# A two-group SSD encoder layer on one core: order of the early loads, 14 more raw tiles in h's own space, ada visits of four

## Chip, cores, metric

The kernel runs on one core of one Trainium2 chip. The metric is device time in microseconds, the median of the timed runs: 3281.73 us for the kernel before (three runs, 3269.22 to 3285.26). All arithmetic is float32; the large matmuls split each operand into a float32r part and a rest and run three products.

## What is computed

One adaLN-modulated mixer layer for 256 prompt rows and 32 sample rows (288 rows, N), D = 4096. Cut to what matters:

```python
mod = silu(c) @ w_ada + b_ada                    # w_ada 4096 x 12288
shift, scale, gate = split(mod, 3)
h = layer_norm(x) * (1 + scale) + shift
proj = h @ w_in                                  # w_in 4096 x 18528
u_pool, g_pool, z, xbc, dt_raw = split(proj)
pool_out = pool_mixer(u_pool) * silu(g_pool)
xs, B, C = split(silu(causal_conv(xbc)))
y = ssd_scan(xs, softplus(dt_raw + dt_bias), A, B, C) + d_skip * xs
ssd_out = grouped_rms_norm(y * silu(z)) * ssd_norm_w
o = concat(pool_out, ssd_out) @ w_out            # w_out 8192 x 4096
x_new = layer_norm(alpha * x + gate * o) * ln_g + ln_b
```

Outputs are x_new for both row groups and the new states of pool, convolution and SSD.

## The kernel before

Everything is transposed: features lie on partitions, the 288 rows are the moving columns. A weight tile of 128 x 128 is stationary, h (or the mixed activations) moves. `hH` and `hL` [128, 32, 288] hold the float32r part and the rest of h, k-tile by k-tile.

Weights come in steps of 512 KB (128 x 1024 floats) into raw tiles, from a first-in-first-out list `rawfree`: four of `rawS` for the whole kernel and five of `rawA` for the first phase. `loads()` hands a free raw tile to the next step in the list and issues its load on SyncE's queue (SP); where the tile's last reader has not finished yet, SP waits there, in order. A w step is converted by ScalarE (`hi`, three buffers), then VectorE computes the rest (`lo`, two buffers) and gives the raw tile back; PE then runs, for each of four blocks of 128 columns and each k-tile, three matmuls hi x hH, hi x hL, lo x hH. An ada step is used raw: c is the stationary operand, w_ada moves.

In the first phase (phase A) h doesn't exist as a whole. It is made in ten slabs of k-tiles, `SLABS = [2]*4 + [4]*6`. Slab s needs its columns of shift and scale, 16 ada steps for a slab of two and 32 for a slab of four (L416 loads them), then `h_slab` (L576): x rows again from memory (L580, L574), normalised by VectorE, transposed by PE, modulated into `ht`, split into `hH` and `hL`. With them the slab's part of 13 blocks of w_in (set A, 49 column tiles) is accumulated into 49 slots of `arena`. Lines 683 to 697 interleave the ada steps of the slabs to come with the w steps: FIRST steps ahead, due LEAD = 4 w steps before a slab begins, in visits of VISIT = 4 ada steps, or of two while the first two slabs run. Before a slab's first w step the program waits in its building (`flush`) for `h_done`. After phase A the full h is there, and the rest of w_in, the pool and SSD work and w_out follow.

The order of instructions on every engine is the order in which the program is built. `run()` (L319) walks the steps; a planner (`tick`) advances background generators between steps, and inside a generator `yield n` means: not before n ticks. For the step at t, conversions are emitted for w steps up to t + 5 + VISIT (L328). `finish` (in `ada_steps`) takes the ada accumulator out by ScalarE (`ev`), sums it by PE (`pR`) and adds b_ada on VectorE (`mod`). At the start twelve loads of x feed 24 `bn_stats`; `x_done` (L561) runs `ln_stats` and `params`, which transposes the parameters that ScalarE's queue loaded ahead of everything else.

Nearly all instructions are issued through one helper and carry the line L101 in the trace; they are told apart by their tiles.

Of the kernel before, what the change touches and what calls it, by code (L numbers as in the profile page):

```python
# [9 lines left out]
F32 = mybir.dt.float32  # L10
# [145 lines left out]
def trunk(ctx, tc, A):  # L156
# [10 lines left out]

    hH = cp.tile([P, KT, N], F32R, name="hH")
    hL = cp.tile([P, KT, N], F32R, name="hL")
    arena = cp.tile([P, NSLOT, N], F32, name="arena")  # L170
# [19 lines left out]
    def pbank(tag):  # L190
        return ps.tile([P, 512], F32, tag=tag, name=tag)
# [37 lines left out]
    def bg(g):  # L229
        pending.append(Gen(g))  # L230
# [71 lines left out]

    rawA_ids = set()

    def raw_free(st):
        if st.rawid in rawA_ids and state.get("noA"):
            return
        rawfree.append((st.rawid, st.raw))
# [3 lines left out]
    def loads():  # L312
        while state["load"] < len(steps) and rawfree:
            st = steps[state["load"]]
            st.rawid, st.raw = rawfree.popleft()
            st.custom(st.raw)
            state["load"] += 1

    def run():  # L319
        for t, st in enumerate(steps):  # L320
            if st.pre:
                st.pre()
            if st.kind != "a" or not steady[0]:
                tick()
            loads()
            ahead = 0
            i = t
            while i < min(state["load"], t + 5 + VISIT) and ahead < HB:  # L328
                if steps[i].kind == "w":
                    if steps[i].hi is None:  # L330
                        split_hi(steps[i])
                    if steps[i].lo is None and ahead < LB:
                        split_lo(steps[i])
                    ahead += 1
                i += 1
            loads()
            T.t = max(T.t, 1.46 * t)
            st.pe(st)
            if st.kind != "w":
                raw_free(st)  # L340
            if st.after:
                st.after()
# [28 lines left out]
    def hmv(kt):  # L371
        return hH[:, kt % KT, :], hL[:, kt % KT, :]

# [91 lines left out]
    def ini(rows, n):  # L465
        inis.append(Slot(free.popleft()))
        return inis[-1].ap[0:rows, 0:n]
# [3 lines left out]
    S.dma_start(c2[32:64, :], A["c_sample"].rearrange("o (k c) -> (o k) c", c=P))  # L471
    p4 = ini(P, P)
    S.dma_start(p4[0:48, :], A["ssd_norm_w"].rearrange("o (k c) -> (o k) c", c=P))
    S.dma_start(p4[48:64, :], A["pool_scale"].rearrange("o (k c) -> (o k) c", c=P))
    S.dma_start(p4[64:96, :], A["ln_g"].rearrange("o (k c) -> (o k) c", c=P))
    S.dma_start(p4[96:128, :], A["ln_b"].rearrange("o (k c) -> (o k) c", c=P))
    ba = ini(96, P)
    S.dma_start(ba, A["b_ada"].rearrange("o (k c) -> (o k) c", c=P))
    cw = ini(P, 2 * P).rearrange("p (a c) -> p a c", a=2)
    S.dma_start(cw, A["conv_w"].rearrange("o r (t c) -> (o r t) c", c=P).rearrange("(a p) c -> p a c", p=P))  # L480
    cb = ini(64, P)
    S.dma_start(cb, A["conv_b"].rearrange("o (t c) -> (o t) c", c=P))
    sv = ini(96, 2 * P).rearrange("p (a c) -> p a c", a=2)
    S.dma_start(sv, A["state_conv"].rearrange("o b r (t c) -> (o b r t) c", c=P).rearrange("(a p) c -> p a c", p=96))
    sp = ini(120, 2 * P).rearrange("p (a c) -> p a c", a=2)
    S.dma_start(sp, A["state_pool"].rearrange("o b r (t c) -> (o b r t) c", c=P).rearrange("(a p) c -> p a c", p=120))
    S.dma_start(sc96[:, 0:1], A["dt_bias"].rearrange("o h -> h o"))
    S.dma_start(sc96[:, 1:2], A["a_log"].rearrange("o h -> h o"))
    S.dma_start(sc96[:, 2:3], A["d_skip"].rearrange("o h -> h o"))

    pt = pbank("pT")
# [3 lines left out]
    V.scalar_tensor_tensor(th, th, 1.0, pt[:, 0:64], ALU.add, ALU.mult)  # L495
    V.tensor_scalar(cT.rearrange("p k s -> p s k"), th.rearrange("p (s k) -> p s k", s=2), 0.5, None, ALU.mult)
    def params():
        pt = pbank("pR")
        T.transpose(pt[:, 0:P], p4, ident)
        T.transpose(pt[:, P:P + 96], ba, ident[0:96, 0:96])  # L500
        V.tensor_copy(prm, pt[:, 0:P])
        V.tensor_copy(badaT, pt[:, P:P + 96])
        V.tensor_scalar(prm[:, 48:64], prm[:, 48:64], 0.5, None, ALU.mult)
        pt = pbank("pY")
        T.transpose(pt[:, 0:128], cw[:, 0, :], ident)
        T.transpose(pt[:, 128:256], cw[:, 1, :], ident)
        T.transpose(pt[:, 256:320], cb, ident[0:64, 0:64])
        T.transpose(pt[:, 320:416], sv[:, 0, :], ident[0:96, 0:96])
        T.transpose(pt[:, 416:512], sv[:, 1, :], ident[0:96, 0:96])
        cvf = convT.rearrange("p r t -> p (r t)")  # L510
        V.tensor_scalar(cvf[:, 0:320], pt[:, 0:320], 0.5, None, ALU.mult)
        V.tensor_copy(cvf[:, 320:512], pt[:, 320:512])
        pt = pbank("pT")
        T.transpose(pt[:, 0:120], sp[:, 0, :], ident[0:120, 0:120])
        T.transpose(pt[:, 120:240], sp[:, 1, :], ident[0:120, 0:120])
        V.tensor_copy(spT.rearrange("p r t -> p (r t)"), pt[:, 0:240])
        for sl in inis:
            sl.rel()
# [24 lines left out]
    def ln_stats():  # L543
        tmp = pa.tile([P, 3, 4], F32, name="lnt")
        for i, (src, rows) in enumerate(xsrc):
            r = slice(0, rows)
            V.bn_aggr(stats[r, i, :], bst[r, i, :, :])
            v, q, y, w = (tmp[r, i, k:k + 1] for k in range(4))
            rs = stats[r, i, 1:2]
            V.tensor_scalar(v, rs, LN_EPS, None, ALU.add)  # L550
            S.activation(q, v, AF.Sqrt)
            V.reciprocal(y, q)
            V.tensor_tensor(w, y, y, ALU.mult)
            V.tensor_tensor(w, w, v, ALU.mult)
            V.tensor_scalar(w, w, -0.5, 1.5, ALU.mult, ALU.add)
            V.tensor_tensor(rs, y, w, ALU.mult)

        for r in (32, 64, 96):
            V.tensor_copy(stats[r:r + 32, 2, :], stats[0:32, 2, :])

    def x_done():  # L561
        ln_stats()
        params()

# [5 lines left out]

    def sample_rows(t, k0, nk):

        for q in range(nk):
            nc.sync.dma_start(t[NS * q:NS * q + NS, :], A["x_sample"][0][:, (k0 + q) * P:(k0 + q + 1) * P])  # L574

    def h_slab(k0, nk):  # L576
        xc = pa.tile([P, 2, 512], F32, tag="xc", bufs=1, name="xc")
        xq = pa.tile([P, P], F32, tag="xq", bufs=1, name="xq")
        for i, (src, rows) in enumerate(xsrc[0:2]):
            nc.sync.dma_start(xc[:, i, 0:nk * P], src[:, k0 * P:(k0 + nk) * P])  # L580
        sample_rows(xq, k0, nk)
        yield
        for i in range(2):
# [7 lines left out]
        for tg in ("pT", "pY"):  # L591
            yield from lock(tg)
        hq = pa.tile([P, P], F32, tag="hq", bufs=1, name="hq")
        for q in range(nk):
# [10 lines left out]
            V.tensor_scalar(ht[:, NP:N], hq[:, NS * q:NS * q + NS], mod[:, 32 + kt, 1:2], mod[:, kt, 1:2], ALU.mult, ALU.add)  # L605
            S.copy(hH[:, kt, :], ht)
            V.tensor_tensor(hL[:, kt, :], ht, hH[:, kt, :].bitcast(F32), ALU.subtract)
            if q % 2:
# [47 lines left out]
    for s, nk in enumerate(SLABS):  # L656
# [7 lines left out]

        def pre(k0=k0, nk=nk):
            bg(h_slab(k0, nk))
        SL[0].pre = pre
        astream += SL
        need.append((len(wstream), len(astream)))
# [12 lines left out]

    early = need[2][0]
    a = paced = need[0][1] + FIRST
    steps.extend(astream[:a])
    for i, w_ in enumerate(wstream):
        steps.append(w_)
        want, due = paced, a
        for w0, a1 in [x for x in need if x[0] > i][:2]:
            left = w0 - LEAD - i  # L690
            want = max(want, a1 if left <= 0 else paced + (a1 - paced) / (left + 1))
            due = max(due, a1 if left <= 0 else 0)
        paced = want
        visit = 2 if i < early else VISIT
        upto = max(due, a + int(paced - a) // visit * visit)
        steps.extend(astream[a:upto])
        a = upto
# [3 lines left out]
    def noA():  # L701
        state["noA"] = True
        keep = [r for r in rawfree if r[0] not in rawA_ids]
        rawfree.clear()
        rawfree.extend(keep)
    st = steps[steps.index(lastA[0]) - 10]
# [557 lines left out]
    def mix_split(kt):  # L1264
        sl = mload.pop(kt)
        q = kt % KT
        S.copy(hH[:, q, :], sl.ap)
        V.tensor_tensor(hL[:, q, :], sl.ap, hH[:, q, :].bitcast(F32), ALU.subtract)
        sl.rel()
# [302 lines left out]
```

## Time and profile before

| | us |
|---|---|
| median of three timed runs | 3281.73 |
| the profiled execution, its time | 3289.41 |
| the profiled execution, span from first to last instruction | 3287.6 |
| PE busy / VectorE / ScalarE / GpSimd | 3139.0 / 1910.2 / 1306.8 / 122.5 |
| mean granted TensorE clock | 0.989 |
| bytes moved | 718.29 MB, 218 GB/s in the mean |

All times in the trace count from the start of the span. PE is TensorE's matmul side, DVE VectorE, ACT ScalarE, POOL GpSimd, SP SyncE; a name with q is the engine's queue, where DMAs are issued. Busy times are spans of instructions; matmuls overlap in the engine, so a group's mean is longer than what one adds. In the chain of waits, x24 on a piece is the number of instructions in it.

### The profile page before, as it was taken

To read this page: it belongs to the slowest core of one execution; us is meant where nothing else is said; L and a number is where in the kernel's file an instruction comes from. 1 tells how busy PE (TensorE), PEld (TensorE's weight loads), DVE (VectorE), ACT (ScalarE), POOL (GpSimd) and SP (SyncE) were. 2 spreads that over 40 slices of the span, in tenths; PEclk is the share of its full clock that TensorE was granted. 3 is DMA by queue.
4 is the path that set the end of the run, shared out by engine and by line. 5 is a ranking of instruction groups with operands and counts; after the bars stand their busy time and mean duration, and the time that the engine had idled before them with its cause. 6 is when DMAs were issued, how large, how long until landed. Compare 5 with 4: busy or idle time off the path is not lost.

```text
span 3287.6 us, 59637 instructions
## 1 busy us (share of the span) xinstructions
PE 3139.0 (95%) x24003; PEld 2911.8 (89%) x24003; DVE 1910.2 (58%) x3335; ACT 1306.8 (40%) x1953; POOL 122.5 (4%) x232
## 2 busy tenths in 40 slices
PE   4988999999999999999999999999899999999998
PEld 1866888888999999999999999989799999999998
DVE  3555555555767746655667656566555533554764
ACT  1422222222434434444444544444444433533543
POOL 0000000000000000000000000000000000000000
PEclk9999999999999999999999999999999999999999
DMA  8878888888565666666666766666766666755554
GB/s 273 287 253 294 312 296 296 299 297 282 149 188 172 200 200 190 197 215 199 212 199 199 217 207 204 197 191 197 230 192 223 205 202 203 244 183 167 170 167 135
DMA packets 428883, 718.29 MB, mean 218 GB/s; under 512 B 34335, under 2 KB 135151, under 8 KB 428607
## 3 DMA queue, kind: packets, MB, share of 16 engines
q1 hardware_dynamic: 418432, 696.39, 66.3%
q0 software_dynamic: 8480, 17.38, 1.4%
q8 instruction: 188, 3.08, 0.4%
q10 hardware_dynamic: 1695, 0.72, 0.1%
q14 instruction: 88, 0.72, 0.1%
HBM read 693.21 MB, written 21.06 MB: 217 GB/s over the span
## 4 chain that ended last, share of the span: by engine, by line
PE 84%; DVE 6%; DMA 6%; ACT 2%; issue 2%; SPq 1%; ACTq 0%; POOL 0%; DVEq 0%; POOLq 0%
PE acc L101 75%; PE ada L101 4%; PE pT L101 3%; DVE lo L101 2%; DMA rawS<-w_in 2%; PE pY L101 2%; DMA rawA<-w_in 1%; DVE arena L101 1%; PE pR L101 1%; DVE cacc L101 1%; ACT hi L101 1%; DMA arena<-spill 1%; DVE ht L101 1%; ACT hH L101 1%; DMA xq<-x_sample 0%
## 5 line engine op out<-in xcount | busy, mean ns | idle before, releaser
L101 PE MATMUL acc<-hH,hi 128*128 128x288 f32 x6688 | 2006.2, 300 | 40.3 <-DVE arena L101 35.9
L101 PE MATMUL acc<-hH,lo 128*128 128x288 f32 x6688 | 1983.9, 297 | 32.3 <-DVE lo L101 31.7
L101 PE MATMUL acc<-hL,hi 128*128 128x288 f32 x6688 | 1981.7, 296 | 0.1
L101 PEld LDWEIGHTS acc<-hH,hi 128*128 128x128 f32 x6688 | 1265.8, 189 | 143.3 <-ACT hi L101 56.1
L101 DVE TENSOR_TENSOR lo<-rawS,hi 128x1024 fp32r<-128x1024 f32 x751 | 914.3, 1218 | 808.6 <-PE acc L101 476.1
L101 PEld LDWEIGHTS acc<-hH,lo 128*128 128x128 f32 x6688 | 1265.0, 189 | 39.6 <-DVE lo L101 38.4
L101 ACT CAST hi<-rawS 128x1024 fp32r<-128x1024 f32 x751 | 784.5, 1046 | 1291.5 <-PE acc L101 570.4
L101 PEld LDWEIGHTS acc<-hL,hi 128*128 128x128 f32 x6688 | 1266.3, 189 | 1.0 <-DVE hL L101 0.5
L101 DVE TENSOR_TENSOR arena<-acc,arena 128x288 f32<-128x288 f32 x441 | 190.4, 454 | 109.9 <-PE acc L101 109.3
L101 ACT CAST hi<-rawA 128x1024 fp32r<-128x1024 f32 (+2 forms) x99 | 99.9, 1011 | 263.1 <-DMA rawA<-w_in 162.0
L101 PE MATMUL ada<-rawS,cT 128*2 128x512 f32 (+1 forms) x1076 | 162.4, 563 | 27.2 <-ACT ev L101 15.9
L101 DVE TENSOR_TENSOR lo<-rawA,hi 128x1024 fp32r<-128x1024 f32 (+2 forms) x99 | 116.2, 1174 | 114.5 <-ACT hi L101 42.6
L101 PE MATMUL ada<-rawA,cT 128*2 128x512 f32 (+1 forms) x716 | 113.5, 539 | 8.1 <-DMA rawA<-w_ada 4.6
L101 ACT ACTIVATE m<-m 128x896 f32<-128x896 f32 x96 | 91.5, 953 | 56.4 <-DVE m L101 54.7
L101 DVE SCALAR_TENSOR_TENSOR cacc<-cbuf,convT,cacc 128x291 f32<-128x291 f32 x192 | 100.3, 522 | 6.8
L101 DVE TENSOR_TENSOR arena<-arena 128x288 f32<-128x288 f32 (+1 forms) x224 | 100.0, 454 | 5.6 <-ACT arena L101 0.7
L101 PEld LDWEIGHTS ada<-rawS,cT 128*2 128x2 f32 x1076 | 21.8, 83 | 63.9 <-issue 27.3
L101 ACT COPY arena<-acc 128x288 f32<-128x288 f32 x177 | 63.9, 403 | 32.7 <-PE acc L101 32.6
L101 ACT ACTIVATE arena<-arena 128x288 f32<-128x288 f32 (+1 forms) x89 | 38.8, 442 | 73.1 <-DVE arena L101 73.0
L101 PE MATMUL pT<-cst,arena 128*128 128x128 f32 (+5 forms) x237 | 46.0, 281 | 18.3 <-DMA arena<-ln_b 6.9
L101 DVE TENSOR_TENSOR hL<-arena,hH 128x288 fp32r<-128x288 f32 x64 | 26.9, 456 | 59.5 <-ACT hH L101 59.4
L101 PEld LDWEIGHTS ada<-rawA,cT 128*2 128x2 f32 x716 | 18.3, 84 | 45.5 <-issue 21.8
(198 smaller groups left out, 1459.1 us busy)
## 6 DMA issues: line engine op xcount, KB each, us to landing
rawS<-w_in SPq DMA_DIRECT2D x426, 512.0 KB, 4.5
rawS<-w_out SPq DMA_DIRECT2D x256, 512.0 KB, 3.7
rawS<-w_ada SPq DMA_DIRECT2D x241, 512.0 KB, 4.4
rawA<-w_ada SPq DMA_DIRECT2D x143, 512.0 KB, 5.5
rawA<-w_in SPq DMA_DIRECT2D x86, 512.0 KB, 6.1
rawS<-w_in SPq DMA_DIRECT2D x114, 256.0 KB, 3.7
m<-acd SPq DMA_DIRECT2D x48, 448.0 KB, 5.0
spill<-arena POOLq DMA_DIRECT2D x64, 144.0 KB, 4.2
```

Source lines behind the costliest of these rows:

```text
L101: return f(out, *a, **k)
```

## The change

Six things are changed.

1. hH and hL become eight tiles each, of four k-tiles. Until a group of k-tiles is made, its space serves as raw tiles: 14 more in `rawfree` (groups 1 to 7, two each). `retire` takes those of groups that the coming slab needs out of the list when the slab's first ada step comes up, and `h_slab` waits in building until they are out of use.
2. Parameters that only later work needs are loaded by GpSimd's queue in a background generator `params`, queued at the last ada step of slab 1, into four arena slots. At the start ScalarE issues only the constants and c; b_ada is loaded and transposed in `params_first`, after the statistics.
3. The x rows of each slab are loaded by GpSimd's queue and first touched six ticks later rather than one.
4. Before the first w step conversions are emitted only up to t + 3.
5. Visits of four ada steps in all slabs.
6. `ln_stats` computes the three row groups' factors at once.

```diff
-    hH = cp.tile([P, KT, N], F32R, name="hH")
-    hL = cp.tile([P, KT, N], F32R, name="hL")
+    early = {(nm, b): cp.tile([P, 4 * N], F32, tag="%s%d" % (nm, b), name="e%s" % nm)
+             for b in range(KT // 4) for nm in ("hH", "hL")}
+    made = {}
+    def hpart(nm, kt):
+        b = kt // 4
+        if (nm, b) not in made:
+            made[nm, b] = cp.tile([P, 4, N], F32R, tag="%s%d" % (nm, b), name=nm)
+        return made[nm, b][:, kt % 4, :]
...
     def raw_free(st):
-        if st.rawid in rawA_ids and state.get("noA"):
+        inuse.discard(st.rawid)
+        if st.rawid in retired:
             return
...
+    def retire(ids):
+        retired.update(ids)
+        keep = [r for r in rawfree if r[0] not in retired]
+        rawfree.clear()
+        rawfree.extend(keep)
...
-            while i < min(state["load"], t + 5 + VISIT) and ahead < HB:
+            while i < min(state["load"], t + (5 + VISIT if t >= state["first"] else 3)) and ahead < HB:
...
-    p4 = ini(P, P)
-    S.dma_start(p4[0:48, :], A["ssd_norm_w"].rearrange("o (k c) -> (o k) c", c=P))
...
-    S.dma_start(sc96[:, 2:3], A["d_skip"].rearrange("o h -> h o"))
...
+    def params_first():
+        ba = ini(96, P)
+        S.dma_start(ba, A["b_ada"].rearrange("o (k c) -> (o k) c", c=P))
+        pt = pbank("pR")
+        T.transpose(pt[:, P:P + 96], ba, ident[0:96, 0:96])
+        V.tensor_copy(badaT, pt[:, P:P + 96])
...
     def params():
+        pi = []
+        for _ in range(4):
+            sl = yield from galloc()
+            pi.append(sl)
...
+        G.dma_start(p4[0:48, :], A["ssd_norm_w"].rearrange("o (k c) -> (o k) c", c=P))
...
+        yield 8
+        yield from lock("pR")
         pt = pbank("pR")
         T.transpose(pt[:, 0:P], p4, ident)
...
     def x_done():
         ln_stats()
-        params()
+        params_first()
...
+    for b in range(1, 8):
+        for q, nm in enumerate(("hH", "hL")):
+            rawfree.append((200 + 2 * b + q, early[nm, b][:, 0:1024]))
...
-            nc.sync.dma_start(xc[:, i, 0:nk * P], src[:, k0 * P:(k0 + nk) * P])
-        sample_rows(xq, k0, nk)
-        yield
+            G.dma_start(xc[:, i, 0:nk * P], src[:, k0 * P:(k0 + nk) * P])
+        sample_rows(xq, k0, nk, G)
+        yield 6
...
+        while any(200 <= i < 200 + 2 * ((k0 + nk + 3) // 4) for i in inuse):
+            yield "w"
...
         def pre(k0=k0, nk=nk):
+            retire([i for b in range(8) if 4 * b < k0 + nk + 2 for i in (200 + 2 * b, 201 + 2 * b)])
             bg(h_slab(k0, nk))
         SL[0].pre = pre
+        if s == 1:
+            SL[-1].pre = lambda: bg(params())
...
-        visit = 2 if i < early else VISIT
-        upto = max(due, a + int(paced - a) // visit * visit)
+        upto = max(due, a + int(paced - a) // VISIT * VISIT)
```

## Rows read from the trace of the kernel before

**Rows 1.** The page, part 1: busy us (share of the span) x instructions of each engine.

```profile
PE 3139.0 (95%) x24003; PEld 2911.8 (89%) x24003; DVE 1910.2 (58%) x3335; ACT 1306.8 (40%) x1953; POOL 122.5 (4%) x232
```

**Rows 2.** Windows: busy us of PE, PEld, DVE, ACT, POOL; then clock, DMA share, GB/s.

```profile
72.00:312.00 240.00, 215.22 (x1692) 178.42 (x1692) 128.10 (x237) 74.15 (x120) 0.00 (x0) 0.94 0.84 278
...
411.00:511.00 100.00, 96.71 (x738) 82.64 (x737) 55.54 (x90) 28.59 (x32) 0.00 (x0) 1.00 0.87 300
...
1000.00:1500.00 500.00, 489.32 (x3728) 465.27 (x3728) 321.45 (x615) 223.65 (x368) 26.35 (x49) 0.99 0.64 197
```

**Rows 3.** Timeline to 72 us: start, us, engine, instruction [idle before <- releaser].

```profile
6.91 0.34 PE L101 MATMUL pT<-cst,arena 64*128 64x64 f32 x1 [6.91 <-DMA arena<-ln_b]
...
13.61 1.28 ACT L101 ACT_TABLE_LOAD   x1 [13.61 <-DMA arena<-state_pool]
...
15.53 4.84 DVE L101 BATCH_NORM_STATS2 bst<-rawS 128x6 f32<-128x512 f32 x8
...
25.92 1.03 PE L101 MATMUL ada<-rawS,cT 128*2 128x256 f32 x8 [9.82 <-DVE bst L101]
...
48.77 1.03 PE L101 MATMUL ada<-rawS,cT 128*2 128x256 f32 x8 [0.48 <-DMA rawS<-w_ada]
...
62.14 1.04 ACT L101 CAST hi<-rawA 128x1024 fp32r<-128x1024 f32 x1 [5.43 <-DMA rawA<-w_in]
...
63.09 0.37 ACT L101 COPY ev<-ada 128x256 f32<-128x256 f32 x1
...
71.98 0.40 PE L101 MATMUL acc<-hH,hi 128*128 128x288 f32 x1 [2.48 <-ACT hH L101]
```

**Rows 4.** Windows of five microseconds with the DMA engines full, columns as above.

```profile
45.00:50.00 5.00, 3.73 (x32) 0.32 (x24) 0.00 (x0) 0.00 (x0) 0.00 (x0) 1.00 1.09 362
...
365.00:370.00 5.00, 5.00 (x42) 4.83 (x44) 2.42 (x4) 2.10 (x2) 0.00 (x0) 1.00 1.05 401
```

**Rows 5.** Waits of SP's queue, 72 to 312 us: total us, times, longest.

```profile
SPq L392 <- DVE lo L101: 68.8, 21, 7.7
SPq L392 <- DVE arena L101: 29.9, 12, 4.2
```

**Rows 6.** The chain of waits in phase A: start, us, what.

```profile
82.86 0.97 PE ada L101 x16
83.83 6.54 PE acc L101 x48
...
177.96 6.33 DMA xc<-x_prompt
...
221.95 6.48 DMA rawA<-w_in
...
307.36 0.27 ACT hq L101
...
312.55 3.44 PE acc L101 x24
```

**Rows 7.** DMA issues: engine, count, KB each, median us to landing.

```profile
spill<-arena POOLq DMA_DIRECT2D x64, 144.0 KB, 4.2
...
arena<-conv_w ACTq DMA_DIRECT2D x1, 128.0 KB, 6.4
...
arena<-b_ada ACTq DMA_DIRECT2D x1, 48.0 KB, 3.8
```

**Rows 8.** Windows inside the stretch of 72 to 312 us.

```profile
165.00:190.00 25.00, 18.02 (x133) 16.83 (x133) 15.20 (x32) 5.33 (x8) 0.00 (x0) 0.92 0.67 214
...
215.00:235.00 20.00, 11.29 (x79) 8.19 (x79) 8.20 (x19) 5.33 (x8) 0.00 (x0) 0.88 0.87 298
```

**Rows 9.** Windows around the x rows' arrival, slabs of four: the first two and the last of five.

```profile
320.00:332.00 12.00, 8.85 (x61) 7.45 (x54) 6.03 (x10) 2.18 (x3) 0.00 (x0) 0.88 0.85 283
...
420.00:436.00 16.00, 14.46 (x108) 12.60 (x109) 10.02 (x19) 3.58 (x4) 0.00 (x0) 1.00 0.87 295
...
721.00:737.00 16.00, 13.02 (x97) 11.16 (x98) 9.38 (x16) 3.57 (x4) 0.00 (x0) 1.00 0.77 250
```

More of the change, by code (lines that the diff above doesn't have):

```diff
@@ L303, in trunk @@
     rawA_ids = set()
+    retired = set()
+    inuse = set()
     def raw_free(st):
-        if st.rawid in rawA_ids and state.get("noA"):
+        inuse.discard(st.rawid)
+        if st.rawid in retired:
             return
@@ L315, in loads @@
             st.rawid, st.raw = rawfree.popleft()
+            inuse.add(st.rawid)
             st.custom(st.raw)
             state["load"] += 1
+    def retire(ids):
[3 more added lines that the diff above has]
+        rawfree.extend(keep)
     def run():
@@ L371, in hmv @@
     def hmv(kt):
-        return hH[:, kt % KT, :], hL[:, kt % KT, :]
+        return hpart("hH", kt % KT), hpart("hL", kt % KT)
     def w_src(w, r0, nk, c0, nc_):
@@ L471, in trunk @@
     S.dma_start(c2[32:64, :], A["c_sample"].rearrange("o (k c) -> (o k) c", c=P))
-    p4 = ini(P, P)
-    S.dma_start(p4[0:48, :], A["ssd_norm_w"].rearrange("o (k c) -> (o k) c", c=P))
[L474 to L488, printed above, removed]
-    S.dma_start(sc96[:, 2:3], A["d_skip"].rearrange("o h -> h o"))
     pt = pbank("pT")
@@ L496, in trunk @@
     V.tensor_scalar(cT.rearrange("p k s -> p s k"), th.rearrange("p (s k) -> p s k", s=2), 0.5, None, ALU.mult)
-    def params():
+    def params_first():
[4 more added lines that the diff above has]
+        V.tensor_copy(badaT, pt[:, P:P + 96])
+        for sl in inis:
+            sl.rel()
+    def params():
+        pi = []
+        for _ in range(4):
+            sl = yield from galloc()
+            pi.append(sl)
+        p4 = pi[0].ap[:, 0:P]
+        cb = pi[0].ap[0:64, P:2 * P]
+        cw = pi[1].ap[:, 0:2 * P].rearrange("p (a c) -> p a c", a=2)
+        sv = pi[2].ap[0:96, 0:2 * P].rearrange("p (a c) -> p a c", a=2)
+        sp = pi[3].ap[0:120, 0:2 * P].rearrange("p (a c) -> p a c", a=2)
+        G.dma_start(p4[0:48, :], A["ssd_norm_w"].rearrange("o (k c) -> (o k) c", c=P))
+        G.dma_start(p4[48:64, :], A["pool_scale"].rearrange("o (k c) -> (o k) c", c=P))
+        G.dma_start(p4[64:96, :], A["ln_g"].rearrange("o (k c) -> (o k) c", c=P))
+        G.dma_start(p4[96:128, :], A["ln_b"].rearrange("o (k c) -> (o k) c", c=P))
+        G.dma_start(cb, A["conv_b"].rearrange("o (t c) -> (o t) c", c=P))
+        G.dma_start(cw, A["conv_w"].rearrange("o r (t c) -> (o r t) c", c=P).rearrange("(a p) c -> p a c", p=P))
+        G.dma_start(sv, A["state_conv"].rearrange("o b r (t c) -> (o b r t) c", c=P).rearrange("(a p) c -> p a c", p=96))
+        G.dma_start(sp, A["state_pool"].rearrange("o b r (t c) -> (o b r t) c", c=P).rearrange("(a p) c -> p a c", p=120))
+        G.dma_start(sc96[:, 0:1], A["dt_bias"].rearrange("o h -> h o"))
+        G.dma_start(sc96[:, 1:2], A["a_log"].rearrange("o h -> h o"))
+        G.dma_start(sc96[:, 2:3], A["d_skip"].rearrange("o h -> h o"))
+        yield 8
+        yield from lock("pR")
         pt = pbank("pR")
         T.transpose(pt[:, 0:P], p4, ident)
-        T.transpose(pt[:, P:P + 96], ba, ident[0:96, 0:96])
+        yield
         V.tensor_copy(prm, pt[:, 0:P])
-        V.tensor_copy(badaT, pt[:, P:P + 96])
+        unlock("pR")
         V.tensor_scalar(prm[:, 48:64], prm[:, 48:64], 0.5, None, ALU.mult)
+        yield
+        yield from lock("pY")
         pt = pbank("pY")
@@ L509, in params @@
         T.transpose(pt[:, 416:512], sv[:, 1, :], ident[0:96, 0:96])
+        yield
         cvf = convT.rearrange("p r t -> p (r t)")
@@ L512, in params @@
         V.tensor_copy(cvf[:, 320:512], pt[:, 320:512])
+        unlock("pY")
+        yield
+        yield from lock("pT")
         pt = pbank("pT")
@@ L515, in params @@
         T.transpose(pt[:, 120:240], sp[:, 1, :], ident[0:120, 0:120])
+        yield
         V.tensor_copy(spT.rearrange("p r t -> p (r t)"), pt[:, 0:240])
-        for sl in inis:
+        unlock("pT")
+        for sl in pi:
             sl.rel()
@@ L543, in ln_stats @@
     def ln_stats():
-        tmp = pa.tile([P, 3, 4], F32, name="lnt")
+        tmp = pa.tile([P, 4, 3], F32, name="lnt")
         for i, (src, rows) in enumerate(xsrc):
[L546 to L556, printed above, removed]
+            V.bn_aggr(stats[0:rows, i, :], bst[0:rows, i, :, :])
         for r in (32, 64, 96):
             V.tensor_copy(stats[r:r + 32, 2, :], stats[0:32, 2, :])
+        v, q, y, w = (tmp[:, k, :] for k in range(4))
+        rs = stats[:, :, 1]
+        V.tensor_scalar(v, rs, LN_EPS, None, ALU.add)
+        S.activation(q, v, AF.Sqrt)
+        V.reciprocal(y, q)
+        V.tensor_tensor(w, y, y, ALU.mult)
+        V.tensor_tensor(w, w, v, ALU.mult)
+        V.tensor_scalar(w, w, -0.5, 1.5, ALU.mult, ALU.add)
+        V.tensor_tensor(rs, y, w, ALU.mult)
     def x_done():
         ln_stats()
-        params()
+        params_first()
     steps[-1].after = x_done
@@ L569, in trunk, with sample_rows @@
         rawA_ids.add(100 + i)
-    def sample_rows(t, k0, nk):
+    for b in range(1, 8):
+        for q, nm in enumerate(("hH", "hL")):
+            rawfree.append((200 + 2 * b + q, early[nm, b][:, 0:1024]))
+    def sample_rows(t, k0, nk, eng=None):
         for q in range(nk):
-            nc.sync.dma_start(t[NS * q:NS * q + NS, :], A["x_sample"][0][:, (k0 + q) * P:(k0 + q + 1) * P])
+            (eng or nc.sync).dma_start(t[NS * q:NS * q + NS, :], A["x_sample"][0][:, (k0 + q) * P:(k0 + q + 1) * P])
     def h_slab(k0, nk):
@@ L605, in h_slab @@
             V.tensor_scalar(ht[:, NP:N], hq[:, NS * q:NS * q + NS], mod[:, 32 + kt, 1:2], mod[:, kt, 1:2], ALU.mult, ALU.add)
-            S.copy(hH[:, kt, :], ht)
-            V.tensor_tensor(hL[:, kt, :], ht, hH[:, kt, :].bitcast(F32), ALU.subtract)
+            hH, hL = hmv(kt)
+            S.copy(hH, ht)
+            V.tensor_tensor(hL, ht, hH.bitcast(F32), ALU.subtract)
             if q % 2:
@@ L680, in trunk @@
         k0 += nk
-    early = need[2][0]
     a = paced = need[0][1] + FIRST
     steps.extend(astream[:a])
+    state["first"] = len(steps)
     for i, w_ in enumerate(wstream):
@@ L701, in noA @@
     def noA():
[L702 to L705, printed above, removed]
+        retire(rawA_ids)
     st = steps[steps.index(lastA[0]) - 10]
@@ L1266, in mix_split @@
         q = kt % KT
-        S.copy(hH[:, q, :], sl.ap)
-        V.tensor_tensor(hL[:, q, :], sl.ap, hH[:, q, :].bitcast(F32), ALU.subtract)
+        hH, hL = hmv(q)
+        S.copy(hH, sl.ap)
+        V.tensor_tensor(hL, sl.ap, hH.bitcast(F32), ALU.subtract)
         sl.rel()
```

## Prediction

> **What bounds the kernel now.** I read the page first. TensorE (PE) is busy for 95% of the span, VectorE 58%, ScalarE 40% [rows 1], so what is not PE work has to show as a hole in PE or as PE at the lower clock. The windows then separate two parts of the span. From about 920 us on nothing of the change is at work except the split of hH into eight tiles. Before that lies phase A: ten slabs of h, w_ada and w_in interleaved, and every engine in its program order. The reader should see two regimes in it. Between 411 and 511 us (one slab of four k-tiles) PE is busy for 96.7 of 100 us [rows 2]. Between 72 us (first accumulation of slab 0) and 312 us (slab 4 begins) it is busy for only 215.2 of 240 us, at a mean granted clock of 0.94 [rows 2]. The clock has two levels, 1.2 and 2.4 GHz, so a mean of 0.94 is 0.06 x 240 = 14 us of work lost besides the 24.8 us of idleness: 39 us lost in this stretch.
>
> The timeline of the first 72 us shows a third piece: w_ada's 16 steps for slab 0 are through PE by 49.8 us (the last group starts at 48.77), but ScalarE takes the ada result out only at 63.09 us, because two conversions "hi" stand ahead of it in ScalarE's order and wait for w_in, the second starting at 62.14; the first accumulation goes at 71.98 [rows 3].
>
> Last I ask whether the DMA engines are the limit. In five-microsecond windows they move 362 GB/s (45 to 50 us) and 401 GB/s (365 to 370 us) [rows 4]; over the slab at 411 us it is 300 GB/s with 0.87 of the engines busy [rows 2]. So they can do more than they are asked for. What asks too little is SP's queue: in the stretch of 72 to 312 us it waits for a raw tile to come free, 68.8 us behind VectorE's "lo" for w_in loads and 29.9 us behind its evictions, as the two largest of seventeen rows [rows 5]. Nine raw tiles are too few there, and each late load shows up in the chain of waits, as 6.48 us for a w_in tile, and as 6.33 us for the x rows, which are queued on SP behind loads that wait for a tile [rows 6].
>
> **The change part by part.**
>
> *Start.* Of ScalarE's issues ten go away ahead of its first activation. ScalarE comes to its table load only at 13.61 us; the first bn_stats starts at 15.53 and 8 take 4.84 us, 0.605 each [rows 3]. After: ScalarE is free some ten issues earlier, the transpose of c goes at 6.91 already now [rows 3], so bn_stats can begin near 8.3; 24 x 0.605 = 14.5 us give 23 us, x landing a little earlier. The batched statistics cost about 3 us, then ScalarE issues b_ada, 3.8 us to landing [rows 7], and the transpose of it holds PE's ada steps until about 30 us. That is later than the 25.92 at which they begin now [rows 3], but nothing is lost: about eight steps lie ready, PE needs 1.03 us for each, and the 16th still ends at 46 to 50 us, as the bytes (4.7 MB of x by about 19 us, then 20 steps of 0.524 MB at 362 GB/s) need until about 48 us, now as before. What changes is the order: with a look-ahead of three steps ahead of the first w step, no "hi" stands ahead of the eviction, which goes at 47 to 50 instead of 63.09. Then pR, transposes and the chain hq, ht, hH take 3 to 4 us: first accumulation at 51 to 54, I take 53, against 71.98. **Gain 19 us** (bounds 15 and 23).
>
> *Fourteen more raw tiles* (12 from slab 1's ada on, 10, 8, 6, 4, 2, 0 later). They remove the waits for a tile in slabs 0 to 3. What PE loses there, in windows: 165 to 190 us 7.0 idle, clock 0.92; 215 to 235 us 8.7, 0.88 [rows 8]; the other 9 us are spread over 195 us. Not all of it is load. At each slab's beginning PE needs h at once, and the chain from hq over ht, hH and hL to the first "lo" stands exposed whatever the loads do: 5.2 us at slab 4's beginning, 307.36 to 312.55 [rows 6], and 4 to 5 at two more. I count 16 us of the idleness and 7 of the 14 us of clock as load. **Gain 23 us** (bounds 12 and 35). The new limit is the DMA: up to slab 4's first w step 83 MB are needed (x 4.7, 96 ada steps 50.3, eight k-tiles of w_in 25.6, x rows again and parameters 2.5); PE could be there at 53 + 240 - 39 + 16 = 270 us, which asks for 310 GB/s, under what [rows 4] shows.
>
> *x rows on GpSimd's queue, looked at six ticks later.* In the slabs of four VectorE comes to xc before the rows have landed, and evictions stand behind it, as at 177.96 in a slab of two [rows 6]. PE's idleness around it is 3.15 us at 320 to 332 (clock 0.88), then 1.54 to 2.98 in four windows of 16 us, first and last shown [rows 9]: 13.3 us with the clock. Part of it is the "lo" of the new slab queued behind the four ht and hL, which stays. **Gain 10 us** (bounds 4 and 13). GpSimd's own cost: six issues of 0.53 us (232 instructions in 122.5 us, [rows 1]) and 4.2 us to landing [rows 7], 7.4 us; six ticks at 57 steps in 100 us are 10.5 us, so the rows are there in time. SP gets rid of as many issues. GpSimd waits for xc alone, with nothing urgent behind it; params' loads are on it once, long before they are needed.
>
> *Late params.* Eight transposes move from an idle PE into a busy one: by the 0.34 us of the transpose of c [rows 3] 2.7 us, some of it under waits that stay. **Cost 2 us** (bounds 0 and 5).
>
> *Visits of four in slabs 0 and 1* halve the number of switches between ada and w; in the chain the accumulations follow a visit of two steps with no gap (82.86 + 0.97 is 83.83) [rows 6], so I take 0 (bounds -3 and 3). *Eight tiles for hH and hL* issue the same instructions; the trace shows no wait that the one tile causes, so 0; a wait of a new writer for an old raw tile could cost a microsecond at a slab's start, since these tiles are out of use some steps before. *After phase A* the order of PE's work is the same and PE is busy there for 489.3 of 500 us [rows 2], so what is won early is kept to the end.
>
> Sum: 19 + 23 + 10 - 2 = 50 us. The profiled execution's span is 3287.6 us and its time 3289.4, 1.8 more; it lies 7.7 us above the median of the timed runs, 3281.7. From the median: **3232 us**.
>
> **The rivals.**
>
> *The x rows come late by GpSimd's queue (slower).* They share the 16 DMA engines with up to 20 tiles of 512 KB that SP has queued. If they had to stand behind these, 20 x 0.524 MB at 362 GB/s are 29 us, 18 us later than VectorE reads them; less some 2 us of cover by lo tiles made ahead, 16 us at nine beginnings are 144 us against the 50 won: 3376 us. It turns slower than before from a landing of about 18 us (50 / 9 = 5.6 above 12.5). Against it: at the start ScalarE's loads landed in 6.4 us at most beside nine full loads of SP's, and GpSimd's in 4.2 us [rows 7]. Chance 0.1. The Trainium skill speaks for this rival (SBUF — State Buffer, section "SBUF: two separate sides"): while VectorE runs an operation in a two-port mode, GpSimd cannot write descriptors, and a transfer that takes 620 ns alone takes about 3100. Six issues at that price would be 19 us and the rows some 12 us late. By that rule the turn to slower is reached; the rows of this case don't show it: GpSimd's instructions take 0.53 us in the mean beside a VectorE that is busy for 58% of the span [rows 1].
>
> *The DMA engines don't sustain more than now.* At the 300 GB/s of [rows 2] the 83 MB need 277 us, slab 4 starts near 283 instead of 312, and a slab of four (57 steps, 30.5 MB) takes 101 us as before: gain 29 - 2, 3255 us. Against it the windows at 362 and 401 GB/s; for it that these are short. Chance 0.13.
>
> *The stalls are of order, not of loads.* Program order of VectorE and ScalarE is set by a planner and stays nearly the same; if the exposed chains and the "lo" behind them are all of it, only the start is won: 19 - 2 = 17, 3265 us. For it speaks that the steady slabs, too, keep SP waiting and PE loses little. Chance 0.12.
>
> *The change does little:* b_ada's load or the loads of x hold PE as long as the "hi" did. 3280 us, chance 0.05.
>
> **How the numbers follow.** My forecast has 0.6. The bounds of its terms together are 28 us less and 25 us more gain: 3207 to 3260. The range takes in the second rival and goes up to the third: 3206 to 3265. 0.5% (16 us) is about what a measurement of this kernel can tell from no change. Faster by more: forecast, second rival and half of the third, 0.8. Within: the other half and the last, 0.1. Slower: 0.1.
>
> **What would show it.** Right: ev's copy and the first accumulation near 50 and 53 us; no hole in the DMA at 50 to 65 us; SP's waits for tiles in slabs 0 to 3 mostly gone and windows at 340 GB/s and more in a row; slab 4 beginning near 270 us; phase A ending about 50 us earlier and everything behind it shifted by as much. Wrong: xc waits in VectorE, GpSimd's loads landing after more than 10 us; PE idle at the same places with tiles to spare; or a stretch after 920 us that has become longer.

## The result, and the profile after

The changed kernel takes 3222.0 us in the median (3219.8 to 3225.1, four runs), the kernel before beside it 3280.7 us: a ratio of 0.983, 95% interval 0.980 to 0.985, 59 us less. Forecast were 3232 us, 50 less.

The profiled execution took 3219.8 us, its span is 3218.0. The page of the changed kernel, part 1, answers to [rows 1]. PE runs the same 24003 instructions, VectorE 12 fewer and ScalarE two fewer (the statistics); of the 69.6 us between the two spans, 40.0 are idleness of PE (148.6 before, 108.6 now) and 29.6 its busy time, at a mean granted clock of 0.994 instead of 0.989.

```profile
PE 3109.4 (97%) x24003; PEld 2899.6 (90%) x24003; DVE 1909.0 (59%) x3323; ACT 1304.7 (41%) x1951; POOL 154.3 (5%) x295
```

Windows of the changed kernel (busy PE, PEld, DVE, ACT, POOL, then clock, DMA share, GB/s). The first runs from slab 0's first accumulation to slab 4's first w step, as 72 to 312 us did in [rows 2]; the second is a slab of four; the third is the first 100 us in which there is w work; the last is all that follows the transposes of slab 9:

```profile
51.40:262.50 211.10, 203.02 (x1701) 172.64 (x1701) 131.96 (x242) 76.40 (x122) 12.13 (x23) 0.99 1.00 351
365.00:465.00 100.00, 97.11 (x741) 83.25 (x741) 56.45 (x94) 28.98 (x33) 3.08 (x6) 1.00 0.85 293
50.00:150.00 100.00, 94.53 (x808) 82.93 (x805) 52.29 (x90) 45.55 (x84) 8.66 (x17) 0.98 1.07 364
753.70:3218.00 2464.30, 2408.01 (x18453) 2307.77 (x18453) 1478.82 (x2581) 1082.75 (x1664) 120.88 (x228) 0.99 0.63 195
```

The same last part of the kernel before:

```profile
813.60:3287.60 2474.00, 2412.83 (x18453) 2312.04 (x18453) 1479.35 (x2581) 1084.13 (x1664) 122.28 (x228) 0.99 0.63 195
```

The stretch of 240 us is now 211, at 351 GB/s instead of 278 and with the DMA engines full. Both last parts hold the same 18453 matmuls.

A table of milestones reads all kernels with one ruler: when the first accumulation starts, and when the transposes of the x rows for h of slab 4 and of slab 9 start on PE (from the timeline). The differences are medians against the kernel before on the same chip. They are known to some 5 to 9 us (the 95% intervals of the ratios are 0.003 to 0.005 wide), and a milestone is read from one execution: e3 and e5, whose edits do nothing behind slab 4, need 1.5 us more than the changed kernel from there to slab 9 (498.5 and 498.4 against 497.0).

| kernel | first accumulation | h of slab 4 | h of slab 9 | median less before |
|---|---|---|---|---|
| before | 71.98 | 306.8 | 813.6 | |
| changed | 51.37 | 256.7 | 753.7 | -58.7 |
| e1_no_tiles | 54.17 | 282.5 | 781.0 | -38.0 |
| e2_tiles_only | 67.77 | 291.4 | 802.0 | -8.1 |
| e4_x_sp | 64.39 | 273.3 | 770.3 | -37.6 |
| e6_yield1 | 51.55 | 260.1 | 758.6 | -58.3 |
| e3_look9 | 59.78 | 260.9 | 759.4 | -54.5 |
| e5_visit2 | 51.34 | 258.7 | 757.1 | -56.4 |
| e7_params_start | 56.03 | 259.1 | 756.1 | -57.6 |
| e11_tiles_queue | 63.08 | 266.8 | 763.7 | -48.1 |
| e8_hsplit | 71.00 | 304.5 | 815.0 | +21.1 |
| e9_tiles6 | 51.41 | 258.1 | 755.0 | -57.7 |

In e10 and e12 some w steps move behind the transposes of their slab, so these milestones don't compare; they stand below. From the first row to the second the gain is 20.6 us at the first accumulation, 50.1 at slab 4, 59.9 at slab 9. Behind that the profiled executions differ by a further 9.7 us; the execution profiled before lay 8.7 us above its median of 3280.7 and the one after 2.2 us below 3222.0, and the medians differ by 58.7, so I count those 9.7 us to the two executions and not to the change.

The start of the changed kernel in the timeline, against [rows 3]:

```profile
8.36 4.84 DVE L101 BATCH_NORM_STATS2 bst<-rawS 128x6 f32<-128x512 f32 x8
...
21.42 1.42 SPq L436 DMA_DIRECT2D ehH<-w_ada  x1
22.60 0.80 DVE L101 BATCH_NORM_AGGREGATE stats<-bst 128x2 f32<-128x48 f32 x3
...
29.77 1.03 PE L101 MATMUL ada<-ehL,cT 128*2 128x256 f32 x8
...
43.71 0.37 ACT L101 COPY ev<-ada 128x256 f32<-128x256 f32 x1 [8.15 <-PE ada L101]
...
44.35 1.03 PE L101 MATMUL ada<-rawA,cT 128*2 128x256 f32 x8 [0.77 <-DMA rawA<-w_ada]
...
45.32 1.02 PE L101 MATMUL pR<-cst,ev 128*128 128x2 f32 x4
...
50.27 1.04 ACT L101 CAST hi<-ehH 128x1024 fp32r<-128x1024 f32 x1
...
51.37 0.40 PE L101 MATMUL acc<-hH,hi 128*128 128x288 f32 x1 [1.02 <-ACT hi L101]
```

ev of the second part is taken at 43.71 instead of 63.09 and no conversion stands ahead of it. SP is still not free of waits in the stretch; the two largest of the changed kernel, 51.4 to 262.5 us (total us, times, longest), answer to [rows 5]:

```profile
SPq L436 <- DVE lo L101: 47.2, 14, 6.8
SPq L436 <- DVE arena L101: 27.4, 12, 4.2
```

All of its waits in the stretch add up to 150 us of 211 (185 of 240 before). It waits now with up to 21 raw tiles given out and not with nine, and PE idles 8.1 us in the stretch instead of 24.8. The x rows and b_ada (DMA issues of the changed kernel up to 764 us: engine, count, KB each, median us to landing) against [rows 7]:

```profile
xc<-x_prompt POOLq DMA_DIRECT2D x12, 256.0 KB, 4.0
xc<-x_prompt POOLq DMA_DIRECT2D x8, 128.0 KB, 5.4
xq<-x_sample POOLq DMA_DIRECT2D x32, 16.0 KB, 4.8
arena<-b_ada ACTq DMA_DIRECT2D x1, 48.0 KB, 5.2
```

### The profile page after: what moved, and what is told of

Same layout as the page of the kernel before. It is cut to its first block, busy times and chain, and to the rows that moved or that the text cites. A ratio compares the mean times of both kernels' runs of the same rounds, so it can differ in the third digit from the quotient of the medians.

```text
span 3218.0 us, 59699 instructions
## 1 busy us (share of the span) xinstructions
PE 3109.4 (97%) x24003; PEld 2899.6 (90%) x24003; DVE 1909.0 (59%) x3323; ACT 1304.7 (41%) x1951; POOL 154.3 (5%) x295
## 4 chain that ended last, share of the span: by engine, by line
PE 87%; DVE 4%; DMA 4%; issue 3%; ACT 2%; SPq 0%; POOL 0%; ACTq 0%; DVEq 0%; POOLq 0%
PE acc L101 77%; PE ada L101 5%; PE pT L101 3%; DMA rawS<-w_in 2%; PE pY L101 2%; DVE lo L101 2%; PE pR L101 1%; DVE ht L101 1%; DMA rawS<-w_out 1%; DVE cacc L101 1%; ACT hH L101 0%; DVE bst L101 0%; ACT hi L101 0%; DVE hL L101 0%; DMA ehH<-w_in 0%
## 5 line engine op out<-in xcount | busy, mean ns | idle before, releaser
L101 DVE TENSOR_TENSOR lo<-rawS,hi 128x1024 fp32r<-128x1024 f32 x730 | 887.8, 1217 | 771.0 <-PE acc L101 459.0
L101 ACT CAST hi<-rawS 128x1024 fp32r<-128x1024 f32 x730 | 761.8, 1045 | 1215.4 <-PE acc L101 597.4
L101 PE MATMUL ada<-rawS,cT 128*2 128x512 f32 (+1 forms) x844 | 122.3, 572 | 1.6 <-DMA rawS<-w_ada 1.6
L101 ACT CAST hi<-rawA 128x1024 fp32r<-128x1024 f32 (+1 forms) x57 | 59.1, 1039 | 138.3 <-PE acc L101 97.3
L101 DVE TENSOR_TENSOR lo<-rawA,hi 128x1024 fp32r<-128x1024 f32 (+1 forms) x57 | 68.9, 1208 | 53.4 <-issue 43.4
L101 ACT COPY arena<-acc 128x288 f32<-128x288 f32 x177 | 63.5, 402 | 29.5 <-PE acc L101 29.5
L101 PE MATMUL ada<-rawA,cT 128*2 128x512 f32 (+1 forms) x460 | 70.9, 557 | 2.3 <-DMA rawA<-w_ada 2.3
L1120 POOL DMA_DIRECT2D new_ssm_prompt<-arena x48 | 26.1, 544 | 738.2 <-ACT arena L101 738.2
L101 ACT CAST hi<-ehL 128x1024 fp32r<-128x1024 f32 (+2 forms) x35 | 35.5, 1014 | 62.3 <-PE acc L101 60.2
```

What stands on the lines that cost most here:

```text
L101: return f(out, *a, **k)
L1120: G.dma_start(A["new_ssm_prompt"][0, 0, ha:ha + 2].rearrange("e p n -> (e p) n"), so[:, 0, :])
```

## Experiments

**Without the tiles.** The edit:

```diff
-    for b in range(1, 8):
-        for q, nm in enumerate(("hH", "hL")):
-            rawfree.append((200 + 2 * b + q, early[nm, b][:, 0:1024]))
```

> The changed kernel without the 14 raw tiles in h's space; all else as changed. If the tiles are what lifts slabs 0 to 3 (my theory): first accumulation stays at 51 to 55 us, slab 4 begins near 287 instead of 262, SP waits again for tiles, the DMA falls from 351 to about 300 GB/s in that stretch; time near 3250 us. If the stalls were of order (rival): slab 4 stays near 265, time within 5 us of 3222.

3246.9 us, 38.0 below the kernel before: 21 us of the 59 are gone. Slab 4's transposes come at 282.5, its first w step at 288.3. The window from the first accumulation to there, and SP's two largest waits:

```profile
54.20:288.30 234.10, 211.60 (x1700) 180.10 (x1701) 130.28 (x242) 75.10 (x121) 12.14 (x23) 0.95 0.88 297
```

```profile
SPq L436 <- DVE lo L101: 59.5, 19, 8.1
SPq L436 <- DVE arena L101: 50.8, 18, 4.2
```

The DMA is down to 297 GB/s, PE idles 22.5 us instead of 8.1, and its mean clock is 0.95 instead of 0.99, which is some 10 us more of work lost. The stretch is 23.0 us longer than in the changed kernel. With the x rows on their own queue, the lateness of the loads is the cause of most of what slabs 0 to 3 lose, as forecast. From slab 4 to slab 9 the kernel without the tiles needs 498.5 us, the changed one 497.0, the one before 506.8: there the tiles give almost nothing.

**The tiles alone**, in the kernel before (its x rows on SP, one tick ahead):

```diff
+    for b in range(1, 8):
+        for q, nm in enumerate(("hH", "hL")):
+            rawfree.append((200 + 2 * b + q, early[nm, b][:, 0:1024]))
...
+            retire([i for b in range(8) if 4 * b < k0 + nk + 2 for i in (200 + 2 * b, 201 + 2 * b)])
             bg(h_slab(k0, nk))
```

> The kernel before with the 14 raw tiles alone (and the eight tiles of h that they need): parameters at the start, x rows on SP one tick ahead, the long look-ahead, visits of two. If late loads are the cause: w_in lands by about 50 us, the two conversions ahead of ev no longer hold it until 63, first accumulation near 58, slab 4 near 275, time near 3245. If order is the cause: first accumulation stays near 70, slab 4 near 305, time over 3270.

3276.8 us, only 8.1 below (ratio 0.9975, 0.996 to 0.999). The first expectation fails (slab 4's transposes come at 291, the time is not 3245). The second has the time right, over 3270, but not the cause: the second ev goes at 57.41 instead of 63.09, and the first accumulation still comes only at 67.77. The waits of VectorE up to 830 us, of this kernel and then of the kernel before, show what took the gain:

```profile
DVE xc L101 <- DMA xc<-x_prompt: 65.9, 15, 24.7
```

```profile
DVE xc L101 <- DMA xc<-x_prompt: 29.0, 12, 6.1
```

In the changed kernel there is no such row. More raw tiles let SP run further ahead with weights, and the x rows, issued in program order on the same queue, stand behind all of them.

**The x rows back on SP**, in the changed kernel, six ticks kept:

```diff
-            G.dma_start(xc[:, i, 0:nk * P], src[:, k0 * P:(k0 + nk) * P])
-        sample_rows(xq, k0, nk, G)
+            nc.sync.dma_start(xc[:, i, 0:nk * P], src[:, k0 * P:(k0 + nk) * P])
+        sample_rows(xq, k0, nk)
         yield 6
```

> The changed kernel with the x rows of the slabs back on SP's queue, still first touched six ticks later. If the queue matters (they stand on SP behind loads that wait for a tile): xc waits on VectorE of some 2 us a slab come back, phase A ends 5 to 10 us later, time near 3230. If the six ticks did it: time within 3 us of 3222.

3247.3 us, 37.6 below the kernel before and so 21 behind the changed one, where I had expected some 8, and at another place: 13.0 us are lost by the first accumulation, 3.6 more by slab 4, none from there to slab 9 (497.0 us). That is 16.6 of the 21; the rest is within what the medians leave open. The first slab's x rows in SP's timeline and VectorE's, in this kernel:

```profile
39.03 7.04 SPq L436 DMA_DIRECT2D rawA<-w_ada  x5
46.17 1.11 SPq L412 DMA_DIRECT2D ehH<-w_in  x1
...
49.02 1.10 SPq L624 DMA_DIRECT2D xc<-x_prompt  x2
...
57.11 0.74 DVE L101 TENSOR_SCALAR xc<-xc,stats 128x256 f32<-128x256 f32 x2 [22.26 <-DMA xc<-x_prompt]
```

VectorE, with nothing else to do, waits 22 us for rows that SP issues behind 20 loads of w_ada and three of w_in (in the kernel before, behind 11 loads of w_ada). At slab 1 it waits 8.4 us more.

**Touched after one tick**, on GpSimd's queue: `yield` in place of `yield 6`.

> The changed kernel with the x rows on GpSimd's queue touched one tick after their issue instead of six. GpSimd's rows landed in 4 to 5 us after issue, six issues take 3 us: VectorE should now meet them some 5 us too early at each slab, of which 1 to 3 us reach PE at nine slabs: phase A 10 to 20 us later, time near 3235. If the queue itself were late by 15 us or more (the slower rival): over 3300.

3226.6 us, 58.3 below: no difference that the medians show; slab 9's transposes are 4.9 us later and VectorE waits 2.5 us for xc in all. Between slab 4 and 9 it is 498.5 us, with the queue but one tick, and 497.0 with SP and six ticks, against 506.8 before: either of the two removes the wait there, both together no more.

**The long look-ahead** (`t + 5 + VISIT` throughout):

> The changed kernel with the long look-ahead (t + 5 + VISIT) before the first w step, as before the change. If ScalarE's order at the start is a cause of its own: two conversions stand ahead of the second ev again and wait for w_in, which lands near 50 us; ev near 52 instead of 43.7, first accumulation near 59 instead of 51.4, time 5 to 8 us above the changed kernel's. If the early loads alone did it: first accumulation at 51 to 53, time within 3 us of the changed kernel's 59 us below the kernel before.

3229.0 us, 54.5 below: 4 less gain than the change, which the intervals don't tell from none; the milestones do. ScalarE's timeline of this kernel shows the order, three conversions and then ev:

```profile
50.19 1.04 ACT L101 CAST hi<-ehH 128x1024 fp32r<-128x1024 f32 x1 [13.59 <-DMA ehH<-w_in]
51.55 1.04 ACT L101 CAST hi<-ehL 128x1024 fp32r<-128x1024 f32 x1 [0.32 <-DMA ehL<-w_in]
52.92 1.04 ACT L101 CAST hi<-ehH 128x1024 fp32r<-128x1024 f32 x1 [0.33 <-DMA ehH<-w_in]
53.87 0.36 ACT L101 COPY ev<-ada 128x256 f32<-128x256 f32 x1
```

The first accumulation is 8.4 us later, as expected; by the transposes of slab 1 it is 4.2 (100.5 against 96.3), at slab 4 still 4.2, and 5.7 at slab 9. So half of this late start is made up. That the loads went on meanwhile, with the DMA engines full, would explain it; this is argued. In e4, where more x rows came late at slab 1, nothing is made up.

**Visits of two in slabs 0 and 1** (`visit = 2 if i < need[2][0] else VISIT`):

> The changed kernel with visits of two ada steps while the first two slabs run, as before the change. My term for the visits was 0: slab 4 begins within 3 us of 262, time within 4 us of the changed kernel's. If fewer switches were worth something: 5 us or more later.

3227.0 us, 56.4 below; slab 4 2.0 us later, slab 9 3.4: within what I had left for it, too small for the medians, and 1.4 us of the 3.4 arise behind slab 4, where the edit changes nothing.

**Parameters at the start**, loaded by ScalarE's queue and transposed there, as before:

> The changed kernel with all parameters loaded by ScalarE's queue and transposed at the start, as before the change. By my working the statistics end near 30 us instead of 23 but the 16th ada step is bound by its bytes: first accumulation at 51 to 55, and eight transposes come out of slabs 1 and 2 again: time within 4 us of the changed kernel's. If the late parameters are what makes the start: first accumulation near 58 or later and 6 us or more lost.

3225.8 us, 57.6 below. The first accumulation is 4.7 us later, slab 9 2.4. The time can't be told from the changed kernel's.

**Tiles and queue together**, in the kernel before: the tiles as above and

```diff
+            G.dma_start(xc[:, i, 0:nk * P], src[:, k0 * P:(k0 + nk) * P])
+        sample_rows(xq, k0, nk, G)
+        yield 6
```

> The kernel before with the 14 raw tiles and the x rows on GpSimd's queue with six ticks; parameters, look-ahead, visits and statistics as before the change. The tiles alone gave 8 us, all but the tiles some 38. If the tiles need the other queue and the two together carry the change: x waits on VectorE gone, slab 4 near 272, time 45 to 52 us below the kernel before. If it is the start's order that the tiles need: 10 to 25 us below.

3235.3 us, 48.1 below. The first accumulation is still at 63.08 (the old order on ScalarE), but slab 4 comes 40 us earlier than before. The waits for xc are gone. Four fifths of the gain lie in these two parts; the tiles alone give 8, all the parts but the tiles 38.

**Eight tiles for hH and hL and nothing else**, made where they are first used:

```diff
-    hH = cp.tile([P, KT, N], F32R, name="hH")
-    hL = cp.tile([P, KT, N], F32R, name="hL")
+    made = {}
+    def hpart(nm, kt):
+        b = kt // 4
+        if (nm, b) not in made:
+            made[nm, b] = cp.tile([P, 4, N], F32R, tag="%s%d" % (nm, b), name=nm)
+        return made[nm, b][:, kt % 4, :]
```

> The kernel before with hH and hL as eight tiles each and nothing else. My term is 0: every milestone of phase A and the time within 0.3% of the kernel before. If tracking by tile costs or saves waits: the stretch behind phase A changes by more than 5 us.

3302.7 us, 21.1 **above** the kernel before (ratio 1.006, 1.004 to 1.008). No milestone of phase A moves by more than 3 us, PE's order of instructions is the same, and it idles no more than before (141 against 149 us of the span); but every accumulation is a little slower. From the chain of waits, a run of 72 accumulations in a steady slab of this kernel:

```profile
448.50 9.79 PE acc L101 x72
```

In the kernel before and in the changed one:

```profile
450.12 9.71 PE acc L101 x72
```

```profile
470.44 9.71 PE acc L101 x72
```

0.08 us in 72 is 1.1 ns each, and 20064 accumulations by 1.1 ns are 22 us. In four more kernels here whose eight tiles are reserved at the start (`early`: e2, e4, e10, e12) it is 9.71 to 9.72 as well. The loss sits in the matmuls that read the eight tiles. Those on the pool's operands pkH and pkL, which the edit leaves alone, have the same row in this kernel and in the kernel before:

```profile
L101 PE MATMUL acc<-pkH,hi 128*128 128x288 f32 x64 | 19.0, 297 | 0.0
```

What differs is when the tiles are allocated, and so perhaps where they lie in memory; the profile shows no addresses, and that the place is the cause is argued and was not tried.

**Six more raw tiles instead of 14** (`for b in range(5, 8)`):

> The changed kernel with 6 instead of 14 more raw tiles (those of the last three groups). If what counts is some slack for SP's queue: nearly all of the gain stays, slab 4 near 265, time within 6 us of the changed kernel's. If every tile counts in proportion: slab 4 near 271 to 274 and 12 us or more lost, as 14 fewer cost some 25.

3223.9 us, 57.7 below: nothing is lost that the medians show, and slab 9's transposes are 1.3 us later. Some slack is what counts: 15 raw tiles do in the early slabs what up to 21 do. How few would do was not tried.

**h earlier and in pieces** (LEAD = 8, and `yield 4` between pairs of k-tiles), and **LEAD = 8 alone**:

> The changed kernel with ada due eight w steps before a slab instead of four, and four ticks instead of one between the pairs of k-tiles in h_slab, so that lo and evictions come between them. PE still loses 2.4 us at each of five boundaries (VectorE's h work ahead of lo and evictions) and 4 to 6 us at two early ones: if they are of order, 10 to 18 us below the changed kernel, near 3208. If the longer lead only makes the DMA late in slabs 0 to 3: no gain or a loss of 5 us.

> The changed kernel with ada due eight w steps before a slab instead of four, nothing else. It moves h earlier, but the h work still stands in one piece: the 2.4 us at the boundaries between slabs of four move with it, the exposed chains in slabs 2 and 4 go: 4 to 8 us below the changed kernel. If the DMA binds there: no gain.

3231.0 and 3234.0 us, 50.6 and 47.6 below the kernel before: both behind the changed kernel in the median, though the intervals overlap. The 5000th accumulation on hH and hL, which lies behind phase A, starts at 897.1 us in the changed kernel, 6.7 us later in the first of them and 10.9 in the second. Windows of the first of them and one of its conversions:

```profile
50.00:150.00 100.00, 90.26 (x783) 77.63 (x776) 50.42 (x89) 45.29 (x86) 12.41 (x23) 0.97 1.08 367
350.00:750.00 400.00, 395.18 (x2988) 336.12 (x2988) 226.19 (x369) 115.27 (x130) 12.35 (x24) 1.00 0.87 297
```

```profile
61.45 1.04 ACT L101 CAST hi<-ehH 128x1024 fp32r<-128x1024 f32 x1 [7.29 <-DMA ehH<-w_in]
```

The second of them, and the changed kernel for the later stretch (its first 100 us stand above):

```profile
50.00:150.00 100.00, 91.13 (x758) 79.89 (x751) 48.32 (x84) 44.09 (x84) 10.78 (x20) 0.93 1.08 367
350.00:750.00 400.00, 390.27 (x2977) 334.58 (x2975) 224.11 (x367) 114.24 (x128) 12.35 (x24) 1.00 0.86 296
```

```profile
350.00:750.00 400.00, 390.30 (x2983) 333.67 (x2976) 224.64 (x365) 115.08 (x130) 12.32 (x24) 1.00 0.86 295
```

In the steady slabs PE idles 4.8 us instead of 9.7 in four slabs, so spreading h's work does what it should; LEAD = 8 alone leaves 9.7 there. But between 50 and 150 us PE idles 9.7 and 8.9 us instead of 5.5, with LEAD = 8 alone at a mean clock of 0.93 instead of 0.98, while the DMA is as full as before: ada that is due earlier pushes w_in back where bytes are short. One conversion waits 7.3 us for its w_in, where the longest such wait between 52 and 75 us was 3.3 in the changed kernel. The pieces with LEAD = 4 were not tried.

## Why the prediction was right, point by point

*What bounds it.* Slots, not the DMA engines: right. Asked were 310 GB/s, the engines gave 364 over 100 us (the third window above) and 351 over the stretch, with 1.00 of the engines busy; there they are now the limit. The second rival (300 GB/s) is out. One sign of being right did not come: SP's waits for tiles in slabs 0 to 3 were to be mostly gone, and all of SP's waits there are 150 us instead of 185. Their sum doesn't tell what a tile is worth; PE's idleness does. The Trainium skill gives about 358 GB/s as the limit of HBM for one core, half of a stack's 716 (DMA: Bandwidth & Descriptors, section "Specifications"). With one core at work here the measured 364 over 100 us lie slightly above that, and the measurement decides.

*Start, 19 us.* 20.6 at the first accumulation. The bn_stats end at 22.60 (said: 23), ada starts at 29.77 (30), ev goes at 43.71 (47 to 50), the accumulation at 51.37 (53). The early steps are right, though ScalarE is rid of 12 issues and not ten, and b_ada took 5.2 us and not 3.8. That the last time fits is in part luck, as two errors cancel. The sum counted the bytes of 20 ada steps where ev needs 16: by its own rates these are there at 42 us, and ev came 3 to 6 us before its time. And from ev to the accumulation it is 7.7 us, not 3 to 4: pR waits in PE's order behind an ada step for slab 1 (until 45.32), and the first w step's conversion stands behind h on ScalarE (until 50.27). The batched statistics were never taken out alone. The term doesn't count in full either: by e3, of a start later by 8.4 us about half is left at slab 4.

*Tiles, 23 us.* The stretch to slab 4 lost 29.5 us of its 240.6 (240.6 to 211.1). By e1 23.0 of them are the tiles', 14.4 of idleness and the rest mostly clock (16 and 7 were said), and the time without them is 21 us longer. The other 6.5 belong to other parts; e4 puts 3.6 of them on the queue of the x rows. Size right, but the sum treated the terms as independent, and here it was wrong: the tiles alone give 8.1 us, as the x rows then stand behind the loads that the tiles let through. The term for the x rows was counted in the slabs of four alone; with the tiles in, its main place is the start, where e4 loses 13 us, and the early slabs.

*x rows, 10 us.* From slab 4 to slab 9 the change gains 9.8 us, and e11 has all of it with the tiles and the x rows alone. Either the queue or the ticks would have sufficed there (e4, e6).

*Late params, cost 2.* They seem to bring 1 to 2 us instead (e7), less than the medians can tell: 4.7 us at the first accumulation, of which 2.4 are left at slab 9.

*Visits, 0; eight tiles, 0.* Visits of four bring some 2 us by the milestones, not clear of their scatter. For the tiles 0 holds as the change makes them (9.71 us for 72 accumulations, as before); as a statement on eight tiles it was wrong by 21 us (e8), and nothing in the profile of before could show it.

*The sum.* 20.6, 29.5 and 9.8 are 59.9 where 50 were said. The 10 us more are the 6.5 in the stretch to slab 4, 1.6 at the start and the 2 for the parameters. The terms' upper bounds add up to 24 us more, not 25; nothing hangs on it.

*After phase A* nothing moved but the start.

*What stays exposed* was seen rightly: 8.8 us of idleness were by the sum to remain in the stretch, and 8.1 did. At the beginnings of slabs 2 and 4 the chain from hq to the next accumulation still takes 5.2 us. In the chain of waits of the changed kernel, three pieces at slab 2's beginning:

```profile
149.24 0.22 ACT hq L101
...
152.75 1.22 DVE lo L101
...
154.39 5.69 PE acc L101 x41
```

*The slower rival* is out: GpSimd's rows land in 4.0 to 5.4 us in the median (7.2 at most for xc), far from 18. The Trainium skill's rule that VectorE, while in a two-port mode, keeps GpSimd from writing descriptors (SBUF — State Buffer, section "SBUF: two separate sides") leaves no trace here: 295 GpSimd instructions took 154.3 us, 0.52 each, beside a VectorE busy for 59%. How much of that time VectorE spends in such a mode, the profile doesn't tell.

## What to carry to other kernels

Before a ring of buffers is made deeper, look at what else is issued on the queue that fills it: what is small and urgent there can get later by as many loads as the ring gains (the first x rows stood behind 11 loads before, and behind 23 in e4). Price such parts together, not one by one: of the 59 us here the deeper ring alone gave 8, with the small loads on another queue 48. Don't read a ring's worth from how long its queue waits, but from what the engine at its end loses. And a gain at the start can be only partly a gain at the end (half of it in e3).

## What the runs showed of the hardware

The same matmuls in the same order can run at another pitch: 9.79 instead of 9.71 us for 72 accumulations in e8, whose operand tiles are allocated later, 21 us of the kernel; the cause stays open. One core's loads ran at 364 GB/s for 100 us with the DMA engines full. At the start of the changed kernel one issue of a 512 KB load held SP's queue for 0.37 us (at 13.76 and 15.53), and from 19.96 on for 1.42, one every 1.46 us (21.42 above), though the DMA engines were full in both stretches (1.05 of them busy from 13 to 16 us, 1.10 from 20 to 26). 0.524 MB in 1.46 us are 359 GB/s: there SP issues as fast as the bytes move.
